# Embedding products in pairs of tiles, with whole-row stores from ACT's queue and earlier weight loads, in a one-layer hybrid decoder step

## The chip, the core and the metric

The kernel is one program on one core of a Trainium2 chip. The metric is the device time of an execution in microseconds (us): 1110.36 as the median of three runs (1109.34 to 1111.5). The engines are PE (matrix products; its weight loads are shown as PEld), DVE (vector), ACT (scalar, with a queue of its own for starting DMAs), POOL, and SP, which only starts DMAs. Each engine takes its instructions strictly in the order in which the program lists them. An instruction whose input or buffer isn't ready holds up everything behind it on its engine.

## What is computed

```python
h = rms_norm(x, norm_pre);  z = h @ w_in                     # 1024 -> 3584
a_out = silu(sg) * (gelu(u) * (W_s @ layer_norm(gelu(v)) + b))  # "S": chunks of 128 positions
b_out = silu(rg) * group_norm(retention(rotary(q), rotary(k), v))  # "R0", "R1": two heads each
mix = concat(a_out, b_out) @ w_out                            # "C1"
x = x + rms_norm(mix, norm_post)
x = x + sigmoid(x @ w_ple_gate) * (p @ w_ple_proj)            # "C2"; p @ w_ple_proj is "P"
```

There are 16 tiles of 128 prompt tokens and one tile of 64 sample tokens. The embedding p has 256 columns, so the product p @ w_ple_proj of a tile is small: two halves of 512 output columns, each of two blocks of 128 rows of p. Every fp32 operand is split into a rounded part (hi) and the rest (lo), and each block is three products (hi·hi, hi·lo, lo·hi). That is 12 products per prompt tile, each 128x128 by 128x512.

## The kernel before

The program is written as one long list of PE products. A counter goes up with each product, and everything else (loads, splits, copies, stores) is entered in the engines' orders at a given count. Stages follow each other on PE: S (all tiles), then P for the first nine tiles (eight of the prompt and the sample tile), R0 (pairs of tiles, seven groups of 12 products per pair: m1, m5, u2, c12, u3, c21, c11), P for the other eight tiles, R1 (as R0), C1, C2. The two P stretches are spoken of below as the first and the second stage boundary.

Names that matter:

- `z` are four PSUM banks used in turn. Each half of a P tile (6 products) takes one, and ACT copies it out (line 1163). A product into the fifth bank waits for the copy of the first.
- `slot` is a ring of 101 buffers of 2 KB per partition, for weights, operands and results alike. `bt` (function `block_rows`) is a pool of two buffers of 4 KB per partition, used before only in C1.
- A P tile's half is copied to a `slot` buffer P and stored from SP's queue (`store`, 12 products after the copy is entered) to `pleD`, 256 KB each. Its input p comes by one load per tile (line 1117), is cast by ACT (line 1130) and its rest is taken by DVE (line 1132).
- `fill` enters a weight's load some products ahead of its split (`lag`), ACT's rounding (lines 230 and 232) and DVE's rest (lines 239 and 241).
- In S, the v part of a tile goes through gelu (lines 376, 378, 380, 382), statistics (396, 398), POOL (401, 402), a scaling on DVE (404), the norm weight on POOL (406), and then four casts on ACT (420). `sgu_batch` mixes four tiles and stores them with `scatter` (16 small DMAs per batch, 64 KB each).
- Lines 936 and 939 take the products of R0 and R1 out of their banks.
- `cs` holds cosines and sines of a tile, loaded by one DMA per tile (line 1034).

Each DMA, whichever queue starts it, signs off on one of eight counters, taken in turn over the whole program. A DMA waits until the one eight places before it has landed.

Of the kernel before, what the change touches and what calls it, by code (L numbers as in the profile page):

```python
# [12 lines left out]
F32 = mybir.dt.float32  # L13
# [94 lines left out]
def hybrid_step(ctx: ExitStack, tc: tile.TileContext, a: dict):  # L108
# [12 lines left out]
    def name(s):  # L121
        uid[0] += 1
        return f"{s}_{uid[0]}"

    def slot(label, shape, dt=F32):

        return ring.tile(shape, dt, tag="slot", name=name(label))
# [10 lines left out]
    def t1k(shape, dt=F32):  # L138
        return slot("t1", shape, dt)
# [58 lines left out]
    def scatter(dst, src, n, qu=None, lag=LAG_D):  # L198


        def go(q):
            (qu or SY).dma_start(  # L202
                out=dst[q].rearrange("(b c) k r -> c b k r", b=4), in_=src[32 * q : 32 * q + 32]
            )

        for q in range(n // 32):
            st.later(lag + 3 * q, lambda q=q: go(q))
# [180 lines left out]
    def s_post(t, part, bank):  # L388
# [4 lines left out]
        if part == 0:  # L393
# [10 lines left out]
            V.tensor_scalar(out=w, in0=w, scalar1=mv[:, 0:1], scalar2=fc, op0=ALU.subtract, op1=ALU.mult)  # L404
            yield 2
            GP.tensor_tensor(out=w, in0=w, in1=sgu["ln"][0:n], op=ALU.mult)  # L406
            yield 7
            if t == SAMPLE:
                store(a["o_sguv"], w)
                sbatch["v", b] = w  # L410
# [40 lines left out]
    def sgu_batch(b):  # L451
# [22 lines left out]
        for h in range(2):  # L474
            yield 2
            for i in range(2):
                bt = blocks(t2k([P, 512]), [us[h][c][:, i, :] for c in range(2)], P)
                scatter(mixT[4 * b + 2 * h + i][:, :, 0:4, :], bt, P)
                yield 3

    def sgu_sample(uu):
# [352 lines left out]
    class Fast:  # L834
# [4 lines left out]
        def __init__(self, tiles, tab, source, post, begin, order):  # L839
            self.tiles, self.tab, self.source, self.post_, self.begin_ = tiles, tab, source, post, begin  # L840
            self.order = order
            self.sample = tiles[0] == SAMPLE
            self.raw, self.ops = {}, {}
            self.length = (32 if self.sample else 84)
# [176 lines left out]
    class FastR(Fast):  # L1021
# [7 lines left out]
            return (r_vg, r_qk)[part](t, self.pr, src, True)  # L1029

        def load(self):
            for t in self.tiles:
                cs = work.tile([P, P], F32, tag="cs", name=name("cs"), bufs=5)
                SY.dma_start(out=cs[0 : np_(t)], in_=a["cs"][t, 0 : np_(t)])
                ret["cs", t] = cs

        def prep(self):
            if self.sample:
# [68 lines left out]
    class Ple:  # L1107
        first = False

        def __init__(self, t, tab):  # L1110
            self.t, self.tab, self.raw, self.ops = t, tab, {}, {}
            self.length = 8 if t == SAMPLE else 12

        def load(self):
            t = self.t
            self.p = t1k([P, 2, P])[:, :, 0 : np_(t)]
            SY.dma_start(out=self.p, in_=(a["psT"] if t == SAMPLE else a["pT"][t]))

        def prep(self):
            p = self.p  # L1120
            if self.t == SAMPLE:
                pc = t1k([P, 2, P], F32R)
                S.copy(out=pc[:, :, 0:TS], in_=p)
                yield 2
                V.tensor_tensor(out=pc[:, :, TS:P], in0=p, in1=f(pc[:, :, 0:TS]), op=ALU.subtract)
                self.ops["p"] = [(pc,)]
            else:
                z = slot("A", [P, 2, 2, P], F32R)
                ph, pl = z[:, 0], z[:, 1]
                S.copy(out=ph, in_=p)  # L1130
                yield 2
                V.tensor_tensor(out=pl, in0=p, in1=f(ph), op=ALU.subtract)
                self.ops["p"] = [(ph, pl)]

        def begin(self):
            pass
# [4 lines left out]

        def main(self):
            seq = []
            for g in range(2):
                bank = [None]

                def first(bank=bank):
                    self.need("p")
                    bank[0] = zbank()

                mms = main_mms(self.t, _Lazy(self.ops, "p"), self.tab, g, range(2), bank)
                seq += [(lambda c=mms[0], first=first: (first(), c()), None)] + [(c, None) for c in mms[1:]]
                seq[-1] = (seq[-1][0], lambda g=g, bank=bank: st.start(self.post(g, bank[0])))
            return seq

        def post(self, g, bank):
            n = np_(self.t)
            if self.t == SAMPLE:
                out = yield from result_of(self.t, bank)
            else:  # L1160
                yield 1
                out = slot("P", [P, 512])
                S.copy(out=out, in_=bank)
            store(pleD[self.t][:, 512 * g : 512 * g + 512], out[0:n])


    c2 = {}
# [151 lines left out]
    unitsC1 = [Unit("C", [t], tabC1) for t in list(range(12)) + [SAMPLE] + list(range(12, NT))]  # L1319
    unitsC2 = [Fast(p, tabC2, x2T, c2_post, c2_begin, STEADY if 0 < j < 7 else ORDER) for j, p in enumerate(pairs)]  # L1320
    unitsC2.insert(4, Fast([SAMPLE], tabC2, x2T, c2_post, c2_begin, ORDER))
    unitsP = [Ple(t, tabP) for t in order]
    units = unitsS + unitsP[:9] + unitsR0 + unitsP[9:] + unitsR1 + unitsC1 + unitsC2

    begin, c = {}, 0
    for u in units:
# [3 lines left out]
    with tc.manual_schedule(engines={ENG.PE, ENG.SP, ENG.Activation, ENG.DVE, ENG.Pool}):  # L1330
# [42 lines left out]
        first8 = lambda u2: [begin[u2] + 12 * j for j in range(8)]  # L1373
        last = begin[unitsS[-1]]
        fill(stepsP, [last - 20 + 12 * j for j in range(4)])
        fill(stepsR0, [last - 24 * (8 - j) for j in range(8)] + [last + 28 + 10 * j for j in range(20)], 24)
        for j in range(NT // 2):
            st.start(spill_sums(j), 200 + 104 * j)
            st.start(spill_weights(j // 4, j % 4), 240 + 200 * j if j < 4 else 1540 + 90 * (j - 4))
        last = begin[unitsR0[-2]]  # L1380
        fill(stepsR1, [last - 25 * (6 - j) for j in range(6)] + [last + 34 + 10 * j for j in range(22)], 24)
        fill(stepsP, [last + 84 + 8 * j for j in range(4)])
        last = begin[unitsR1[-2]]
        fill(stepsC1, [last - 60 + 20 * j for j in range(5)] + [last + 46 + 8 * j for j in range(11)], 20)
# [142 lines left out]
```

## Time and profile before

| what | value |
|---|---|
| median of 3 runs | 1110.36 us |
| profiled execution | 1108.41 us, span 1106.6 us |
| PE / PEld busy | 1078.3 / 894.3 us (97% / 81%) |
| DVE / ACT / POOL busy | 811.2 / 501.0 / 357.8 us |
| granted clock, mean | 0.993 |
| chain that ended last | PE 86%, DVE 4%, DMA 4% |
| DMA | 253.55 MB, mean 229 GB/s |

In the table, busy is the time in which an engine executes something. The granted clock is TensorE's, as a share of full speed. The span leaves 28.3 us in which PE is not busy; 6.5 us of these lie behind the last product. The rest are a few gaps at the three places where one stage ends and another begins (about 280 to 345, 510 to 570 and 740 to 760 us).

### The profile page before, as it was taken

How to read it: one execution, taken by the hardware profiler on the slowest of the kernel's cores; microseconds unless marked ns; L12 is line 12 of the kernel's file. 1: busy time of each engine (PE TensorE's matmuls, PEld its weight loads, DVE VectorE, ACT ScalarE, POOL GpSimd, SP SyncE). 2: the span in 40 equal slices, each digit the busy share in tenths (PEclk: the TensorE clock that was granted, in tenths of full speed). 3: DMA queues.
4: the chain of work that ended last, by engine and by line, in shares of the span. 5: the costliest groups of instructions: out<-in, count | busy, mean ns of one | idle time of the engine just before them, and what ended most of it. 6: DMA issues, size and time to landing. Idle time of an engine off the chain costs nothing.

```text
span 1106.6 us, 16497 instructions
## 1 busy us (share of the span) xinstructions
PE 1078.3 (97%) x5028; PEld 894.3 (81%) x5028; DVE 811.2 (73%) x1512; ACT 501.0 (45%) x1042; POOL 357.8 (32%) x570
## 2 busy tenths in 40 slices
PE   9999999999898999999899999998999999999997
PEld 7888887888687888887778888886788888888886
DVE  4887687787755677879555666796678888986885
ACT  6664454654653334535543233353333244444442
POOL 5755454655301233333212323343355411000000
PEclk9999999999999999999999999999999999999999
DMA  9754867775597678897886656776768677865854
GB/s 309 242 195 152 290 233 222 258 266 162 186 321 247 220 241 269 287 286 211 271 268 197 193 171 209 233 218 186 228 217 264 190 226 229 268 216 193 282 162 143
DMA packets 227224, 253.55 MB, mean 229 GB/s; under 512 B 39104, under 2 KB 132800, under 8 KB 227136
## 3 DMA queue, kind: packets, MB, share of 16 engines
q1 hardware_dynamic: 217632, 243.85, 68.7%
q10 hardware_dynamic: 9504, 8.65, 2.7%
q8 instruction: 40, 0.66, 0.2%
q14 instruction: 48, 0.39, 0.1%
HBM read 172.86 MB, written 79.56 MB: 228 GB/s over the span
## 4 chain that ended last, share of the span: by engine, by line
PE 86%; DVE 4%; DMA 4%; ACT 2%; SPq 2%; issue 1%; POOL 1%; ACTq 0%; DVEq 0%; POOLq 0%
PE z L212 67%; PE s L212 19%; DMA t<-qkT 2%; SPq L202 1%; DMA W<-w_in 1%; DMA W<-wT 1%; DVE W L239 1%; DMA A<-xS10l 0%; ACT W L230 0%; DMA X<-xT 0%; DVE W L241 0%; POOL t L406 0%; DVE t L194 0%; DVE C L978 0%; DVE C L973 0%
## 5 line engine op out<-in xcount | busy, mean ns | idle before, releaser
L212 PE MATMUL z<-W,A 128*128 128x512 f32 x3632 | 897.7, 396 | 13.4 <-ACT C L936 5.2
L212 PEld LDWEIGHTS z<-W,A 128*128 128x128 f32 x3632 | 682.3, 189 | 155.2 <-ACT C L936 6.5
L212 PE MATMUL s<-W,A 128*128 128x512 f32 x672 | 184.3, 403 | 0.0
L212 PEld LDWEIGHTS s<-W,A 128*128 128x128 f32 x672 | 124.6, 189 | 21.4
L936 ACT COPY C<-z 128x512 f32<-128x512 f32 x96 | 56.2, 586 | 153.8 <-PE z L212 152.2
L529 POOL TENSOR_TENSOR t<-t,t 128x256 f32<-128x256 f32 (+1 forms) x34 | 28.5, 837 | 223.8 <-DVE t L526 103.5
L212 PEld LDWEIGHTS s<-t,t 128*128 128x128 f32 (+1 forms) x400 | 73.6, 186 | 12.4 <-issue 2.7
L212 PE MATMUL s<-t,t 128*128 128x128 f32 (+2 forms) x400 | 76.2, 272 | 0.0
L241 DVE SCALAR_TENSOR_TENSOR W<-W,c_npre,W 128x512 fp32r<-128x512 f32 x48 | 40.0, 845 | 41.2 <-ACT W L232 35.2
L863 DVE TENSOR_TENSOR A<-X,A 128x512 fp32r<-128x512 f32 (+1 forms) x78 | 54.0, 694 | 15.0 <-ACT A L861 14.8
L939 DVE TENSOR_TENSOR C<-z,C 128x512 f32<-128x512 f32 x48 | 33.1, 690 | 42.4 <-ACT C L936 26.7
L194 DVE STREAM_TRANSPOSE t<-t 128x512 f32<-128x512 f32 (+3 forms) x69 | 39.4, 573 | 27.0 <-POOL t L530 15.5
L555 ACT ACTIVATE t<-C,rsall 128x128 f32<-128x128 f32 (+1 forms) x68 | 23.6, 395 | 75.4 <-DVE C L939 68.0
L861 ACT CAST A<-X 128x512 fp32r<-128x512 f32 (+1 forms) x78 | 46.9, 602 | 4.5 <-DMA wT<-W 1.4
L603 POOL TENSOR_TENSOR t<-t,t 128x256 f32<-128x256 f32 (+1 forms) x34 | 29.5, 868 | 51.0 <-DVE t L598 43.0
L290 ACT CAST A<-X 128x512 fp32r<-128x512 f32 (+1 forms) x62 | 37.1, 600 | 19.4 <-issue 5.4
L1182 ACT ACTIVATE C<-C 128x512 f32<-128x512 f32 (+1 forms) x34 | 21.3, 633 | 50.4 <-DVE C L939 47.3
L239 DVE TENSOR_TENSOR W<-W,W 128x512 fp32r<-128x512 f32 x48 | 34.5, 722 | 10.6 <-ACT W L230 10.3
L292 POOL TENSOR_TENSOR A<-X,A 128x512 fp32r<-128x512 f32 (+1 forms) x28 | 39.3, 1424 | 5.2 <-ACT A L290 5.2
L232 ACT ACTIVATE W<-W,c_npre 128x512 fp32r<-128x512 f32 x48 | 33.8, 719 | 14.3 <-DMA W<-w_in 13.2
L422 POOL TENSOR_TENSOR v<-t,v 128x128 fp32r<-128x128 f32 x64 | 33.6, 547 | 16.1 <-ACT v L420 16.1
L380 ACT ACTIVATE t<-t,rsall 128x512 f32<-128x512 f32 (+1 forms) x34 | 24.2, 722 | 31.4 <-DVE t L378 31.4
(143 smaller groups left out, 1351.3 us busy)
## 6 DMA issues: line engine op xcount, KB each, us to landing
X<-xT SPq DMA_DIRECT2D x106, 256.0 KB, 4.2
W<-w_in SPq DMA_DIRECT2D x80, 256.0 KB, 4.9
X<-x SPq DMA_DIRECT2D x64, 256.0 KB, 4.2
qkT<-t SPq DMA_DIRECT2D x132, 64.0 KB, 2.0
x2T<-bt ACTq DMA_DIRECT2D x66, 128.0 KB, 3.7
wT<-W SPq DMA_DIRECT2D x32, 256.0 KB, 4.6
W<-wT SPq DMA_DIRECT2D x32, 256.0 KB, 3.9
ple<-P SPq DMA_DIRECT2D x32, 256.0 KB, 4.7
```

The lines of the kernel that those rows point to most:

```text
L194: V.transpose(out=by_k[:, k : k + nk], in_=part.rearrange("p (k b r) -> p k b r", b=4, r=32))
L212: PE.matmul(out, lhsT=l, rhs=r, start=start, stop=stop, skip_group_check=again)
L232: S.activation(out=hi, in_=raw, func=AF.Copy, scale=sc)
L239: V.tensor_tensor(out=lo, in0=raw, in1=f(hi), op=ALU.subtract)
L241: V.scalar_tensor_tensor(out=lo, in0=raw, scalar=sc, in1=f(hi), op0=ALU.mult, op1=ALU.subtract)
L290: S.copy(out=hi, in_=r)
L292: eng.tensor_tensor(out=lo, in0=r, in1=f(hi), op=ALU.subtract)
L422: GP.tensor_tensor(out=los[q][:, :, t % 4, :], in0=i, in1=f(o), op=ALU.subtract)
L861: S.copy(out=hi, in_=raw)
L863: V.tensor_tensor(out=lo, in0=raw, in1=f(hi), op=ALU.subtract)
L936: S.copy(out=c[key], in_=banks[b])
L939: V.tensor_tensor(out=c[key], in0=banks[b], in1=c[key], op=ALU.add)
```

## The change

Five edits are made together.

1. P works in pairs of tiles: one load, one cast and one subtraction for two tiles (512 KB, 128x512 per instruction). The PE order stays as it was, product for product.
2. The two halves of a P tile are copied into one buffer of the `bt` pool and stored with one DMA of whole rows (512 KB) that ACT's queue starts. The sample tile stays as before.
3. One load of `cs` per pair of tiles (3 buffers of two tiles instead of 5 of one).
4. The weights of R0 and R1 are loaded 40 products ahead instead of 24.
5. In S the four casts of v are entered 14 products after POOL's step instead of 7, and the 16 `scatter` DMAs of the last batch are started by ACT, 30 products after their transposes instead of 12.

```diff
@@ s_post, sgu_batch
-            yield 7
+            yield 14
             if t == SAMPLE:
...
-                scatter(mixT[4 * b + 2 * h + i][:, :, 0:4, :], bt, P)
+                scatter(mixT[4 * b + 2 * h + i][:, :, 0:4, :], bt, P, *((S, 30) if b == 3 else ()))
@@ FastR.load
-            for t in self.tiles:
-                cs = work.tile([P, P], F32, tag="cs", name=name("cs"), bufs=5)
-                SY.dma_start(out=cs[0 : np_(t)], in_=a["cs"][t, 0 : np_(t)])
-                ret["cs", t] = cs
+            t, n, w = self.tiles[0], np_(self.tiles[0]), len(self.tiles)
+            cs = work.tile([P, 2, P], F32, tag="cs", name=name("cs"), bufs=3)
+            SY.dma_start(out=cs[0:n, 0:w], in_=a["cs"][t : t + w, 0:n].rearrange("t p c -> p t c"))
+            for i, t in enumerate(self.tiles):
+                ret["cs", t] = cs[:, i]
@@ Ple
+            self.p = slot("A", [P, 2, 2, P])
+            t = self.tiles[0]
+            SY.dma_start(out=self.p, in_=a["pT"][t : t + 2].rearrange("t p k c -> p t k c"))
...
-                z = slot("A", [P, 2, 2, P], F32R)
-                ph, pl = z[:, 0], z[:, 1]
-                S.copy(out=ph, in_=p)
+                hi, lo = slot("A", [P, 2, 2, P], F32R), slot("A", [P, 2, 2, P], F32R)
+                S.copy(out=hi, in_=p)
                 yield 2
-                V.tensor_tensor(out=pl, in0=p, in1=f(ph), op=ALU.subtract)
-                self.ops["p"] = [(ph, pl)]
+                V.tensor_tensor(out=lo, in0=p, in1=f(hi), op=ALU.subtract)
+                for i, t in enumerate(self.tiles):
+                    self.ops[t] = [(hi[:, i], lo[:, i])]
...
-                out = slot("P", [P, 512])
-                S.copy(out=out, in_=bank)
-            store(pleD[self.t][:, 512 * g : 512 * g + 512], out[0:n])
+            yield 1
+            if g == 0:
+                self.out[t] = block_rows(P)
+            out = self.out[t]
+            S.copy(out=out[:, 512 * g : 512 * g + 512], in_=bank)
+            if g:
+                store(pleD[t], out, S)
@@ main part
-    unitsP = [Ple(t, tabP) for t in order]
-    units = unitsS + unitsP[:9] + unitsR0 + unitsP[9:] + unitsR1 + unitsC1 + unitsC2
+    unitsP = [Ple(p, tabP) for p in pairs]
+    unitsP.insert(4, Ple([SAMPLE], tabP))
+    units = unitsS + unitsP[:5] + unitsR0 + unitsP[5:] + unitsR1 + unitsC1 + unitsC2
...
-        fill(stepsR0, [last - 24 * (8 - j) for j in range(8)] + [last + 28 + 10 * j for j in range(20)], 24)
+        fill(stepsR0, [last - 24 * (8 - j) for j in range(8)] + [last + 28 + 10 * j for j in range(20)], 40)
...
-        fill(stepsR1, [last - 25 * (6 - j) for j in range(6)] + [last + 34 + 10 * j for j in range(22)], 24)
+        fill(stepsR1, [last - 25 * (6 - j) for j in range(6)] + [last + 34 + 10 * j for j in range(22)], 40)
```

ACT's order at the first boundary before, from the copy of the first P half on. A row is a line of the kernel, the operation, result and inputs; in brackets stand the counters that it waits for (PE, DVE, ACT's own, and DMAHW0 to 7, the eight counters of the DMAs).

```order
L1163 COPY P_3559<-z_3539 128x512 [waits PE_49]
L1130 CAST A_3562<-t_665_3481 128x256 [waits DMAHW7_49]
L1163 COPY P_3575<-z_3557 128x512 [waits PE_49,Activation_49]
L232 ACTIVATE W_3582<-W_3522,c_npre 128x512 [waits DMAHW2_49]
L1163 COPY P_3591<-z_3573 128x512 [waits PE_49]
L1130 CAST A_3594<-t_671_3518 128x256 [waits DMAHW1_49,Activation_49]
L1163 COPY P_3606<-z_3586 128x512 [waits PE_49]
L232 ACTIVATE W_3609<-W_3544,c_npre 128x512 [waits DMAHW3_49]
L1163 COPY P_3622<-z_3603 128x512 [waits PE_49]
```

Every copy waits for PE alone, since each has a new buffer of the ring. The same place now, from the third half on (`bt_3582`, `bt_3608` and `bt_3636` are the rows of the second, third and fourth tile; ple_222 is signed off on counter 5, ple_223 on counter 1):

```order
L1172 COPY bt_3582<-z_3566 128x512 [waits PE_49]
L185 DMA ple_222<-bt_3553 128x1024 [waits Activation_49]
L1172 COPY bt_3582<-z_3578 128x512 [waits PE_49]
L232 ACTIVATE W_3594<-W_3499,c_npre 128x512 [waits DMAHW0_49]
L1172 COPY bt_3608<-z_3589 128x512 [waits DMAHW5_49,PE_49]
L1135 CAST A_3611<-A_3538 128x512 [waits DMAHW2_49]
L230 CAST W_3619<-W_3524 128x512 [waits DMAHW1_49]
L185 DMA ple_223<-bt_3582 128x1024 [waits Activation_49]
L1172 COPY bt_3608<-z_3606 128x512 [waits PE_49]
L1172 COPY bt_3636<-z_3623 128x512 [waits DMAHW1_49,PE_49]
```

The stores have moved into ACT's order, each behind the first copy of the tile after next. From the third tile on, the first copy of a tile waits for the landing of the store of the tile two before it.

SP's order at the first boundary before, from the load of the last p of the stretch on:

```order
L1117 DMA t_688_3578<-pT 128x256 [waits DMAHW6_49,PE_49]
L185 DMA ple_222<-P_3559 128x512 [waits DMAHW7_49,Activation_49]
L223 DMA W_3598<-wT_196 128x512 [waits DMAHW0_49,PE_49]
L185 DMA ple_222<-P_3575 128x512 [waits DMAHW1_49,Activation_49]
L1117 DMA t_698_3611<-psT 128x2x64 [waits DMAHW2_49,PE_49]
```

The stores of P stood there among the loads, each waiting for ACT's copy; now there is none of them on SP. ACT's order now where R0 begins (`mixT` are the small DMAs of the last S batch, `C_3889` is the copy of m1's bank):

```order
L202 DMA mixT_104<-t_733_3761 32x4x128 [waits DMAHW1_49]
L202 DMA mixT_105<-t_738_3775 32x4x128 [waits DMAHW2_49]
L232 ACTIVATE W_3882<-W_3767,c_npre 128x512
L202 DMA mixT_106<-t_742_3789 32x4x128 [waits DMAHW3_49]
L202 DMA mixT_107<-t_748_3806 32x4x128 [waits DMAHW4_49,DVE_49]
L202 DMA mixT_105<-t_738_3775 32x4x128 [waits DMAHW5_49]
L936 COPY C_3889<-z_3849 128x512 [waits PE_49,Pool_49]
```

Before, these 16 DMAs stood on SP. Eleven of them now stand on ACT ahead of m1's copy, and five behind it.

## Rows read from the trace of the kernel before

**Rows 1.** Timeline of PE, 255 to 345 us (start, duration, [idle before <-releaser])

```profile
298.16 9.35 PE L212 MATMUL z<-W,A 128*128 128x512 f32 x33 [4.18 <-DVE t L382]
...
323.76 8.32 PE L212 MATMUL z<-W,A 128*128 128x512 f32 x36
333.06 3.01 PE L212 MATMUL z<-W,A 128*128 128x512 f32 x12 [0.97 <-ACT C L936]
338.18 4.62 PE L212 MATMUL z<-W,A 128*128 128x512 f32 x12 [2.10 <-ACT C L936]
```

**Rows 2.** Windows: PE, PEld, DVE, ACT, POOL busy, granted clock, DMA share, GB/s

```profile
280.00:300.00 20.00, 15.82 (x67) 12.74 (x66) 16.71 (x28) 12.72 (x30) 8.63 (x13) 0.95 0.49 169
300.00:320.00 20.00, 20.00 (x97) 16.82 (x96) 14.27 (x37) 12.90 (x27) 0.00 (x0) 0.96 0.92 324
...
520.00:540.00 20.00, 15.46 (x66) 12.05 (x67) 14.30 (x31) 11.91 (x26) 5.15 (x6) 0.91 0.75 215
540.00:560.00 20.00, 17.89 (x80) 14.46 (x79) 8.60 (x23) 9.74 (x18) 3.85 (x8) 0.94 1.02 356
```

**Rows 3.** Timeline of ACT, 270 to 345 us

```profile
295.27 0.30 ACT L420 CAST v<-t 128x128 fp32r<-128x128 f32 x1 [3.18 <-POOL t L406]
295.47 0.72 ACT L380 ACTIVATE t<-t,rsall 128x512 f32<-128x512 f32 x1
...
300.08 0.58 ACT L1163 COPY P<-z 128x512 f32<-128x512 f32 x1
300.56 0.73 ACT L232 ACTIVATE W<-W,c_npre 128x512 fp32r<-128x512 f32 x1
301.19 0.57 ACT L1163 COPY P<-z 128x512 f32<-128x512 f32 x1
...
331.81 0.72 ACT L232 ACTIVATE W<-W,c_npre 128x512 fp32r<-128x512 f32 x1 [4.54 <-DMA W<-w_in]
332.44 0.57 ACT L936 COPY C<-z 128x512 f32<-128x512 f32 x1
```

**Rows 4.** Waits of SP's queue, 280 to 302 us (total, times, longest)

```profile
SPq L185 <- ACT A L1130: 13.3, 1, 13.3
```

**Rows 5.** Timeline of SP, 270 to 345 us

```profile
286.45 0.38 SPq L1117 DMA_DIRECT2D t<-pT  x1
299.90 0.33 SPq L185 DMA_DIRECT2D ple<-P  x1
```

**Rows 6.** Timeline of PE, 540 to 572 us

```profile
556.94 10.09 PE L212 MATMUL z<-W,A 128*128 128x512 f32 x36 [2.11 <-ACT C L936]
```

**Rows 7.** Timeline of ACT, 505 to 575 us

```profile
528.15 0.58 ACT L1163 COPY P<-z 128x512 f32<-128x512 f32 x1
...
553.81 0.41 ACT L543 COPY t<-t 128x256 f32<-128x256 f32 x1 [4.85 <-DMA t<-qkT]
...
556.31 0.58 ACT L936 COPY C<-z 128x512 f32<-128x512 f32 x1
```

**Rows 8.** Timeline of PE, 740 to 765 us

```profile
750.45 0.49 PE L212 MATMUL s<-t 128*128 128x128 f32 x2 [3.34 <-ACT t L543]
```

**Rows 9.** DMA issues, 272.5 to 277 us (operation, count, size, median us to landing)

```profile
xS37h<-A SPq DMA_DIRECT2D x1, 256.0 KB, 2.0
```

**Rows 10.** DMA issues, 524 to 546 us

```profile
ple<-P SPq DMA_DIRECT2D x9, 256.0 KB, 3.3
```

**Rows 11.** DMA issues of the whole span

```profile
ple<-P SPq DMA_DIRECT2D x32, 256.0 KB, 4.7
```

**Rows 12.** Tile bt: DMA issue on ACT's queue (duration in ns, min/median/max)

```profile
L202 ACTq DMA_DIRECT2D x2T<-bt x66: 309/385/758, 767.4 to 953.9; - x66
```

**Rows 13.** Groups by form (count, busy us, mean ns, idle before)

```profile
L420 ACT CAST v<-t 128x128 fp32r<-128x128 f32 x64 | 15.7, 293 | 34.4 <-POOL t L406 34.4
L230 ACT CAST W<-W 128x512 fp32r<-128x512 f32 x48 | 29.5, 618 | 7.5 <-DMA W<-wT 2.9 <-DVE W L239 2.4 <-DMA W<-w_out 1.1
L1130 ACT CAST A<-t 128x256 fp32r<-128x256 f32 x16 | 6.4, 402 | 0.0
```

More of the change, by code (lines that the diff above doesn't have):

```diff
@@ L1108, in hybrid_step, with __init__ @@
         first = False
-        def __init__(self, t, tab):
-            self.t, self.tab, self.raw, self.ops = t, tab, {}, {}
-            self.length = 8 if t == SAMPLE else 12
+        def __init__(self, tiles, tab):
+            self.tiles, self.tab, self.ops, self.out = tiles, tab, {}, {}
+            self.sample = tiles[0] == SAMPLE
+            self.length = 8 if self.sample else 12 * len(tiles)
         def load(self):
-            t = self.t
-            self.p = t1k([P, 2, P])[:, :, 0 : np_(t)]
-            SY.dma_start(out=self.p, in_=(a["psT"] if t == SAMPLE else a["pT"][t]))
+            if self.sample:
+                self.p = t1k([P, 2, P])[:, :, 0:TS]
+                SY.dma_start(out=self.p, in_=a["psT"])
+                return
+            self.p = slot("A", [P, 2, 2, P])
+            t = self.tiles[0]
+            SY.dma_start(out=self.p, in_=a["pT"][t : t + 2].rearrange("t p k c -> p t k c"))
         def prep(self):
             p = self.p
-            if self.t == SAMPLE:
+            if self.sample:
                 pc = t1k([P, 2, P], F32R)
@@ L1125, in prep @@
                 V.tensor_tensor(out=pc[:, :, TS:P], in0=p, in1=f(pc[:, :, 0:TS]), op=ALU.subtract)
[L1126 removed]
+                self.ops[SAMPLE] = [(pc,)]
             else:
[L1128 to L1130 removed]
+                hi, lo = slot("A", [P, 2, 2, P], F32R), slot("A", [P, 2, 2, P], F32R)
+                S.copy(out=hi, in_=p)
                 yield 2
[L1132 to L1133 removed]
+                V.tensor_tensor(out=lo, in0=p, in1=f(hi), op=ALU.subtract)
+                for i, t in enumerate(self.tiles):
+                    self.ops[t] = [(hi[:, i], lo[:, i])]
         def begin(self):
@@ L1143, in main, with first, post @@
             seq = []
[L1144 to L1153, printed above, removed]
-            return seq
[L1156 to L1161, printed above, removed]
-                out = slot("P", [P, 512])
-                S.copy(out=out, in_=bank)
-            store(pleD[self.t][:, 512 * g : 512 * g + 512], out[0:n])
+            for t in self.tiles:
+                for g in range(2):
+                    bank = [None]
+                    def first(t=t, bank=bank):
+                        self.need(t)
+                        bank[0] = zbank()
+                    mms = main_mms(t, _Lazy(self.ops, t), self.tab, g, range(2), bank)
+                    seq += [(lambda c=mms[0], first=first: (first(), c()), None)] + [(c, None) for c in mms[1:]]
+                    seq[-1] = (seq[-1][0], lambda t=t, g=g, bank=bank: st.start(self.post(t, g, bank[0])))
+            return seq
+        def post(self, t, g, bank):
+            if self.sample:
+                out = yield from result_of(t, bank)
+                store(pleD[t][:, 512 * g : 512 * g + 512], out)
+                return
+            yield 1
[5 more added lines that the diff above has]
+                store(pleD[t], out, S)
     c2 = {}
```

## The prediction

> **What bounds the kernel now.** I read the page first. PE is busy for 97% of the span, and the chain that ended last is 86% PE, so only PE's gaps and slow stretches can be won. PE's timeline then showed where they are: at three stage boundaries.
>
> At the first boundary PE stands still three times, for 4.18, 0.97 and 2.10 us [rows 1]. After the first wait 33 products take 9.35 us. The 36 products later take 8.32 us (0.227 each, with 0.17 of tail), so 33 should take 7.5: PE ran part of them at 1.2 GHz, and the granted clock of that window is 0.95 to 0.96 [rows 2]. After the third wait 12 products take 4.62 us, where 12 took 3.01 [rows 1]. Such a low stretch costs 1.6 to 1.9 us behind a wait. At the second boundary the last wait is 2.11 us, and the 36 products behind it take 10.09 us [rows 6]. At the third one wait is 3.34 us [rows 8].
>
> ACT's timeline tells why. The 4.18 us wait is for line 382, whose input comes from the tanh of line 380. That tanh stood behind a cast of line 420 which waited 3.18 us for POOL [rows 3]. Then SP: it issued nothing from 286.45 to 299.90, as its next DMA was the first store of P and waited 13.3 us for ACT [rows 4, 5]. The loads behind it came late: at 331.81 a weight's rounding on ACT had waited 4.54 us for its load, and the copy of R0's bank stood behind it [rows 3]. That is PE's wait of 0.97, and the 2.10 is the same again. At the second boundary a copy of line 543 waited 4.85 us for its load, ahead of m1's copy at 556.31 [rows 7].
>
> **The change part by part.** The change takes away the causes just named: no store of P on SP, the casts of line 420 behind the tanh, loads further ahead. What it puts in their place has to be priced. PE's order is the same, so the sum is a shift of a few points of that order.
>
> *Two row buffers.* A P tile now needs a `bt` buffer from its first copy until its store has landed, and there are two. On ACT, in order: first copy of tile i+2 (waits for the landing of store i), one or two casts, store i+1, second copy of i+2, first copy of i+3 (waits for store i+1), and so on. Store i+1 stands behind the copy that waits for store i, so the landings follow one another and can't overlap: six landings from store 0 to the first copy of tile 7. I call one landing D, from issue to the buffer's release.
>
> First boundary. Before, the third half's copy began at 301.19 [rows 3], and store 0 is now issued right behind it. The tanh of line 380 no longer waits, which moves this row by about 0.6 (0.72 for the tanh that goes first, less what the casts behind it take over): 300.6. Between the landings ACT has 1.5, 1.0, 0.8, 1.5 and 0.5 us of copies and casts that can't be hidden (0.5 each when they follow closely, by the starts 300.08 and 300.56 [rows 3]): 5.3. So tile 7's first copy begins at 300.6 + 5.3 + 6D = 305.9 + 6D. From there to m1's copy ACT has three more copies, two casts, one rounding at 0.63, 13 DMA issues at 0.43 (0.385 and a gap [rows 12]) and the copy itself: 2.0 + 1.0 + 0.6 + 5.6 + 0.6 = 9.8. Eleven of the 13 are the `mixT` DMAs. u2 can't begin before that copy: 315.7 + 6D. Then u2, c12 and u3 at 2.72 each, 0.6 for m5's copy behind five more issues, and one low-clock stretch of 1.9 as after such waits before: u3 ends at 326.4 + 6D. Before, u3 ended at 338.18 + 4.62 = 342.8 [rows 1]. The shift is 6D - 16.4.
>
> Second boundary. Store 0 is issued at 528.7, behind the third copy at 528.15 [rows 7]; nothing ahead of it changes much. Between the landings stand 1.0, 1.0, 1.0, 1.5 and 0.5: tile 7's first copy at 533.7 + 6D. Then two copies, two issues and two roundings, and m1's copy, 3.7 in all: u2 at 537.4 + 6D. Before, u2 began at 556.94 [rows 6], and I let the low clock behind it stand. The shift is 6D - 19.5.
>
> Together 12D - 35.9. It is zero at D = 2.99 us, and every 0.1 us of D is 1.2 us.
>
> *What D is.* No row shows a store of 512 KB. From below: 256 KB landed in 2.0 us with the queues nearly empty [rows 9], so D isn't under 2.0. From above: the median of P's stores is 4.7 us [rows 11], where SP kept the DMAs full (share 0.92 [rows 2]). The nearest row is P's stores at the second boundary, with SP's loads beside them: 3.3 us [rows 10]. The second 256 KB cost 0.7, at the 350 GB/s that 324 GB/s at a share of 0.92 make for a full share [rows 2], so 4.0 if nothing else changed. But in this chain SP is held too, since its eighth DMA behind a store waits for that store; DMAs are emptier than there. I take D = 3.5, nearer to 4.0 than to the idle row's 2.0 + 0.7 = 2.7. The sum is 42.0 - 35.9 = +6.1.
>
> The Trainium skill ("DMA: Bandwidth & Descriptors", section "Anatomy of one DMA") fits a DMA as 2.0 us plus its bytes at 436 GB/s, measured on GpSimd's path: an estimate of 3.2 us for 512 KB and, by the same sum, +2.5 us. For 256 KB it gives 2.6, while the rows here have 2.0 idle and 3.3 to 4.7 loaded, so the trace agrees with it only in the middle. The rule that speaks against the change is in "Perfetto Trace Analysis", section "Identifying the Most-Contended Engine": the same gap again and again on the engine that should be full can mean too few buffers. PE's gaps before are single ones [rows 1, 6]; by that rule the change would make them a row of equal ones, as the forecast has it.
>
> *The rest.* 16 casts of 402 ns become 8 of about 618 [rows 13]: 1.5 us less of ACT, and about as much of DVE, beside waits. 16 loads of cosines, 8 of p and 32 stores fewer on SP, at 0.33 to 0.38 each [rows 5], save some 20 us of a queue that isn't what PE waits for any more at these places. Line 420's 34.4 us of waits [rows 13] are hidden by the z banks everywhere but at the 4.18 wait. Loads 40 products ahead hold ring slots 16 products (3.6 us) longer; the 20 buffers that P no longer takes from the ring at each boundary (12 for 32) cover that. All this I put at nothing, with 1 us either way. The third boundary's 3.34 [rows 8] comes from line 543's chain, which no edit touches.
>
> **Sum.** The profiled execution took 1108.4 us, 2.0 below the median of the runs. 1108.4 + 6.1 = 1114.5, and on the scale of the median 1116.5.
>
> **The rivals.**
>
> A. The stores land early enough, and PE sets the pace. For it: D = 2.7 from the idle row. Then tile 7's copy is ready when PE is. At the first boundary the tanh still leaves some 3 us of the first wait, and the `mixT` issues still hold m1's copy, so 4 to 6 of the waits and low clock go; at the second the 2.11 and its low stretch of 1.8 go. Some -9: 1101.5. Against it: DMA shares of 0.75 to 1.0 at both places [rows 2]. The Trainium skill ("DMA: Bandwidth & Descriptors", section "Rules for kernel authors") has merged transfers pay; by that rule alone A would be the outcome, and no run here has yet shown a store of this size.
>
> B. Worse than the chain: landings couple through the eight counters. SP's loads behind a store wait for it, and weights of R0 or R1 come late again, so that the roundings of rows 3 hold copies up once more. Price: D of 4.2 (+14.5), or the old 0.97 + 2.10 + 1.6 back on top of the forecast: about 1122 to 1125. It decides once a period of the chain moves more than the DMAs do in it: a store and three to five loads are 1.2 to 1.8 MB, 3.5 to 5 us at 350 GB/s, against a period of D + 1.
>
> C. D near 3.0: what the chain costs is what the old waits cost. 1110.
>
> D. The row buffers hardly matter, since the wait of ACT is shorter than the four z banks. Against it: the banks cover 5.4 us once, while the landings add up to 18 us and more over eight tiles that take PE 21.8.
>
> **How the numbers follow.** Forecast (D from 3.2 to 4.0) 0.50, B 0.17, C 0.12, A with D 0.21. Likeliest 1116.5, its own range 1112 to 1122. Taking in most of A and of B, the range is 1102 to 1129. A change of under 0.2% (2.2 us) can't be told from none here. Faster 0.21, same 0.13, slower 0.66.
>
> **What would show it.** In the profile after: ACT copies of line 1172 with DMA `ple<-bt` as the releaser, some 2 to 3 us each and five or six in a row at both boundaries; PE's waits there for that line; `ple<-bt` x16 of 512 KB at 3 to 4 us to landing; SP's long wait and the wait for line 380 gone; m1's copy behind a row of `mixT` issues on ACT. The forecast is wrong if `ple<-bt` lands in under 2.9, if the copies wait for PE alone, or if PE's largest waits lie elsewhere.

## The result, and the profile after

The changed kernel takes 1115.64 us (median of five runs, 1113.75 to 1117.33) against 1109.63 for the kernel before in the same measurement (1107.16 to 1111.5). The ratio is 1.0054, with a 95% interval of 1.0035 to 1.0073: slower by 6.0 us, where 6.1 were forecast. The profiled execution took 1115.95 us with a span of 1114.1, so it lies 7.5 us over the profiled one of before. The total came out as forecast; its parts did not all do so.

First the page of the kernel after: the chain that ended last by lines, PE's largest group with the idle time ahead of it, and the new stores (count, size, median us to landing).

```profile
PE z L212 66%; PE s L212 18%; DMA ple<-bt 3%; DMA W<-w_in 1%; DMA t<-qkT 1%; DMA mixT<-t 1%; DVE W L239 1%; DMA X<-xT 0%; DMA A<-xS46h 0%; DMA cs<-cs 0%; DMA t<-xT 0%; DVE W L241 0%; DVE C L939 0%; DVE C L978 0%; DVE C L973 0%
...
L212 PE MATMUL z<-W,A 128*128 128x512 f32 x3632 | 899.8, 397 | 13.0 <-ACT bt L1172 5.7
...
ple<-bt ACTq DMA_DIRECT2D x16, 512.0 KB, 4.5
```

The stores stand in the chain with 3% of the span, and what PE waits for most in this group is the copy of P's banks. A store lands in 4.5 us, against 4.7 for the halves of before over the whole span [rows 11].

The waits of the kernel after, of PE and then of ACT (total us, times, longest):

```profile
PE s L212 <- ACT t L543: 9.2, 5, 3.3
PE z L212 <- ACT bt L1172: 7.5, 5, 2.5
PE z L212 <- ACT C L936: 3.2, 3, 1.4
PE z L212 <- DVE t L382: 2.4, 1, 2.4
...
ACT bt L1172 <- DMA ple<-bt: 23.4, 9, 3.8
```

The wait for line 382 is 2.41 us where it was 4.18 [rows 1], and the waits for line 936 are shorter. In their place stand 7.5 us for line 1172, behind ACT's 23.4 us for landings. SP's wait of 13.3 us for ACT [rows 4] is gone, but SP isn't free: it now stands for landings of stores, since each DMA waits for the one eight places before it. Its queue's waits that end between 298 and 345 us, the kernel after:

```profile
SPq L1058 <- DMA ple<-bt: 11.6, 3, 4.2
SPq L1054 <- DMA ple<-bt: 9.5, 1, 9.5
SPq L223 <- DMA ple<-bt: 4.2, 1, 4.2
SPq L185 <- DMA ple<-bt: 3.4, 1, 3.4
```

They add up to 28.7 us. The 9.5 us end at 302.46, just behind the landing of the first store, which ACT issued at 299.75; before, SP's long wait ended at 299.90 [rows 5]. Now ACT's timeline at the first boundary after, from store 1 to m1's copy; rows of ACTq are DMA issues.

```profile
303.13 0.59 ACT L1172 COPY bt<-z 128x512 f32<-128x512 f32 x1 [0.24 <-PE z L212]
303.14 0.33 ACTq L185 DMA_DIRECT2D ple<-bt  x1
...
308.01 0.59 ACT L1172 COPY bt<-z 128x512 f32<-128x512 f32 x1 [2.77 <-DMA ple<-bt]
308.12 0.33 ACTq L185 DMA_DIRECT2D ple<-bt  x1
308.50 0.62 ACT L230 CAST W<-W 128x512 fp32r<-128x512 f32 x1
309.01 0.59 ACT L1172 COPY bt<-z 128x512 f32<-128x512 f32 x1
309.49 0.63 ACT L230 CAST W<-W 128x512 fp32r<-128x512 f32 x1
312.69 0.59 ACT L1172 COPY bt<-z 128x512 f32<-128x512 f32 x1 [2.56 <-DMA ple<-bt]
312.79 0.33 ACTq L185 DMA_DIRECT2D ple<-bt  x1
...
326.80 0.59 ACT L1172 COPY bt<-z 128x512 f32<-128x512 f32 x1 [2.99 <-DMA ple<-bt]
...
333.79 0.72 ACT L232 ACTIVATE W<-W,c_npre 128x512 fp32r<-128x512 f32 x1 [3.79 <-DMA mixT<-t]
...
335.34 0.59 ACT L936 COPY C<-z 128x512 f32<-128x512 f32 x1 [0.82 <-DVE W L241]
```

One landing releases one copy, and 0.1 us after the copy starts the next store goes out: 308.12, 312.79, and so on, five times. The casts between them lie inside the wait for the landing, since the copy that waits stands behind them. PE's timeline there, the kernel after:

```profile
297.02 9.47 PE L212 MATMUL z<-W,A 128*128 128x512 f32 x33 [2.41 <-DVE t L382]
...
322.85 2.11 PE L212 MATMUL z<-W,t 128*128 128x512 f32 x8 [1.76 <-ACT bt L1172]
327.44 7.38 PE L212 MATMUL z<-W,A 128*128 128x512 f32 x24 [2.47 <-ACT bt L1172]
335.98 3.04 PE L212 MATMUL z<-W,A 128*128 128x512 f32 x12 [1.16 <-ACT C L936]
339.65 5.74 PE L212 MATMUL z<-W,A 128*128 128x512 f32 x24 [0.63 <-ACT C L936]
```

The rows answer to those of before [rows 1]. The 24 products at 327.44 took 7.38 us where 24 take 5.6 to 5.7, so part of them ran at 1.2 GHz (the granted clock between 320 and 340 us is 0.91); behind 335.98 there is no such stretch. Further on in the kernel after, late in R0, at the second and at the third boundary, PE again:

```profile
506.34 0.71 PE L212 MATMUL s<-t 128*128 128x128 f32 x2 [2.04 <-ACT t L543]
...
526.41 3.49 PE L212 MATMUL z<-W,A 128*128 128x512 f32 x14 [0.69 <-DVE W L239]
...
557.48 5.73 PE L212 MATMUL z<-W,A 128*128 128x512 f32 x24 [0.88 <-ACT bt L1172]
564.65 8.46 PE L212 MATMUL z<-W,A 128*128 128x512 f32 x36 [1.45 <-ACT C L936]
...
756.55 0.79 PE L212 MATMUL s<-t 128*128 128x128 f32 x2 [3.34 <-ACT t L543]
757.85 7.17 PE L212 MATMUL z<-W,A 128*128 128x512 f32 x21
```

In R0 there is a wait of 2.04 us that before did not have, with a low stretch behind it (the pair behind the wait takes 0.71, the one at 750.45 in before 0.49; the granted clock between 506 and 512 us is 0.72). At the second boundary u2 starts 7.7 us later than before [rows 6], but its 36 products take 8.46 and not 10.09. At the third the wait is the same 3.34 us [rows 8]; 21 products behind it take 7.17, where in the timeline of PE before they took 5.04:

```profile
751.15 5.04 PE L212 MATMUL z<-W,A 128*128 128x512 f32 x21
```

### The profile page after: what moved, and what is told of

Read it like the earlier page. It is cut to its first block, busy times and chain, and to the rows that moved or that the text cites. A ratio compares the mean times of both kernels' runs of the same rounds, so it can differ in the third digit from the quotient of the medians.

```text
span 1114.1 us, 16390 instructions
## 1 busy us (share of the span) xinstructions
PE 1082.4 (97%) x5028; PEld 896.0 (80%) x5028; DVE 815.6 (73%) x1504; ACT 500.4 (45%) x1034; POOL 364.0 (33%) x570
## 4 chain that ended last, share of the span: by engine, by line
PE 85%; DMA 8%; DVE 4%; ACT 1%; issue 1%; SPq 0%; ACTq 0%; POOL 0%; DVEq 0%; POOLq 0%
PE z L212 66%; PE s L212 18%; DMA ple<-bt 3%; DMA W<-w_in 1%; DMA t<-qkT 1%; DMA mixT<-t 1%; DVE W L239 1%; DMA X<-xT 0%; DMA A<-xS46h 0%; DMA cs<-cs 0%; DMA t<-xT 0%; DVE W L241 0%; DVE C L939 0%; DVE C L978 0%; DVE C L973 0%
## 5 line engine op out<-in xcount | busy, mean ns | idle before, releaser
L422 POOL TENSOR_TENSOR v<-t,v 128x128 fp32r<-128x128 f32 x64 | 36.3, 596 | 19.1 <-ACT v L420 19.1
```

Of the source, the lines that this page charges most:

```text
L422: GP.tensor_tensor(out=los[q][:, :, t % 4, :], in0=i, in1=f(o), op=ALU.subtract)
```

## Where the time stands, place by place

For each kernel I took six points of PE's timeline that the unchanged order lets one find again: the start of the first wait at boundary 1 (293.98 in before), the first product of two small operands in R0 (354.47), the wait for line 239 at the end of R0 (519.93), the first small product behind boundary 2 (590.48), the wait of 3.34 (750.45) and the end. The table has what each kernel lost (+) or won (-) against the profiled execution of before between two points, in us. It is one execution of each; the runs of one kernel spread over 3 to 8 us (12 in E10), so single entries under 2 us mean little, and columns more than entries.

| kernel | ahead | boundary 1 | R0 | boundary 2 | rest | sum |
|---|---|---|---|---|---|---|
| after | +0.63 | +1.91 | +3.94 | -0.39 | +1.41 | +7.50 |
| E1, lead 24 | +0.25 | +2.91 | -0.03 | +3.84 | +1.63 | +8.60 |
| E2, four row buffers | +0.41 | -0.89 | +5.12 | -2.59 | +2.25 | +4.30 |
| E3, pairs of P alone | -0.03 | +2.64 | +2.17 | +1.35 | +0.47 | +6.60 |
| E4, all but the pairs | +0.13 | -1.07 | +2.57 | -3.87 | +0.64 | -1.60 |
| E5, halves in the ring | +0.62 | -1.86 | +2.00 | -3.30 | +0.54 | -2.00 |
| E6, half-row stores | +0.24 | +1.74 | +3.05 | +1.19 | +0.58 | +6.80 |
| E7, E4 and split lead | +0.27 | -3.78 | +4.13 | -3.47 | -0.25 | -3.10 |
| E8, E4 and 98 slots | +0.41 | -3.18 | +3.29 | -3.07 | +2.05 | -0.50 |
| E9, E4 and lead 24 | +0.22 | -1.18 | +1.34 | -2.21 | +0.23 | -1.60 |
| E10, E6 and mixT on SP | +0.60 | -0.47 | +6.15 | +1.84 | +0.18 | +8.30 |
| E11, E7 and 102 slots | 0.00 | -3.50 | +0.87 | -2.66 | +0.29 | -5.00 |
| E12, E5, split lead, 102 | +0.02 | -3.12 | +4.12 | -3.43 | -0.29 | -2.70 |

What R0's column is made of can be read from the traces. PE's waits of over 0.1 us for line 543 there add up to 1.0 us in before, 0.9 in E1, 3.4 in after and 1.7 to 5.2 in the others. In after, line 543 itself had waited for a load of `qkT`:

```profile
505.67 0.62 ACT L543 COPY t<-t 128x512 f32<-128x512 f32 x1 [3.19 <-DMA t<-qkT]
```

The rest of after's +3.94, about 1.6 us, is the low stretch behind 506. A wait near 499 to 506 us (0.64 to 2.04) stands in all ten kernels that load R0's weights 40 products ahead, and in none of the four with 24 (before, E1, E3, E9). So this wait comes with the longer lead, and what E4 over E9, and after over E1, lose in R0 (1.2 and 4.0 us) they get back at boundary 2 (1.7 and 4.2). An earlier wait, near 475 to 483 us, stands in all fourteen (0.76 to 2.37); why it varies is not shown.

## The experiments

My theory after the result was the forecast's: two row buffers make the landings follow one another, and that is the price. The rival was that the other edits, above all the longer lead, cost what is seen in R0, and that the row buffers are beside the point. Each kernel was timed in five rounds beside the kernel before; us of difference are the ratio less one, times 1109.6. E9 to E12 ran on another chip than E1 to E8, so that the two groups are compared by their ratios alone.

**E1.** The lead of the weights' loads back at 24.

```diff
-... [last + 28 + 10 * j for j in range(20)], 40)
+... [last + 28 + 10 * j for j in range(20)], 24)
-... [last + 34 + 10 * j for j in range(22)], 40)
+... [last + 34 + 10 * j for j in range(22)], 24)
```

> The kernel after with the weights' loads 24 products ahead again. Theory 1 (the longer lead costs in R0): a load of W that waits for a ring buffer stood ahead of the qkT DMAs on SP at 485.59 to 488.18, they came 5 us late, and PE's wait of 2.04 us at 506.34 with the low clock behind it (1.8) follows from that. Then that wait goes and the median is 1115.6 - 3.8 = 1111.8 (1110.8 to 1112.8); the waits of ACT for ple<-bt stay near 23 us. Theory 2 (all of the loss is the two row buffers, and the wait in R0 is only a late start handed on): 1115.6, 0.7 either way, with the wait in place.

Measured: 1115.07 us, ratio 1.0061 (1.0045 to 1.0078). The wait at 506 is gone from its trace, as theory 1 had it, but the time is not: boundary 2 gave the same amount back (+3.84 for -0.39 in the table). R0 ended 3.35 us sooner than in after (523.06 for 526.41), but the landings took longer (28.1 us for the first six at boundary 2, 25.8 in after), and tile 7's first copy came at 561.10 for 561.82. By the time, theory 2 has it, though the wait that it expected in place is gone: the lead makes the wait in R0, but it is no cause of the loss as a whole.

**E2.** Four row buffers for two, and a ring of 98 slots for 101 to make room.

```diff
-SLOTS = 101
+SLOTS = 98
-        return work.tile([P, D], F32, tag="bt", name=name("bt"), bufs=2)[0:n]
+        return work.tile([P, D], F32, tag="bt", name=name("bt"), bufs=4)[0:n]
```

> The kernel after with four row buffers in place of two (ring of 98 slots in place of 101, for the room). Theory 1 (two row buffers make the landings follow one another): ACT's 23.4 us of waits for ple<-bt fall under 3, PE's waits for line 1172 go, u3 ends 3 to 5 us sooner than 345.2, and the time is 1111 to 1113; the wait in R0 stays. Theory 2 (m1's copy is held by the mixT DMAs and by late loads whatever the buffers): 1115, 1 either way.

Measured: 1112.31 us, ratio 1.0029 (1.0017 to 1.0042), 2.8 us better than after, though a store now lands in 5.0 us. Both boundaries are better than before. ACT's waits of line 1172 for a landing are gone; one of 1.7 us, ahead of line 333, is left. PE's waits in this kernel:

```profile
PE s L212 <- ACT t L543: 9.1, 7, 3.4
PE z L212 <- ACT C L936: 5.6, 3, 3.1
PE z L212 <- DVE t L382: 3.6, 1, 3.6
PE z L212 <- ACT bt L1172: 2.4, 2, 1.8
```

The 2.4 us for line 1172 stand ahead of the chain at boundary 2, where after has them too (0.64 and 1.73 at 530 to 534), and none at boundary 1. So the landings still take as long, but they overlap. What is left of the loss stands in R0, and E8 shows that the smaller ring costs by itself.

**E3 and E4.** The pairs of P with their row buffers alone, and all other edits without them.

E3, against before (with the rest of class `Ple` as in the change):

```diff
-    unitsP = [Ple(t, tabP) for t in order]
+    unitsP = [Ple(p, tabP) for p in pairs]
...
+                store(pleD[t], out, S)
```

E4, against before (with both lines of `fill`):

```diff
-            yield 7
+            yield 14
...
-                scatter(mixT[4 * b + 2 * h + i][:, :, 0:4, :], bt, P)
+                scatter(mixT[4 * b + 2 * h + i][:, :, 0:4, :], bt, P, *((S, 30) if b == 3 else ()))
...
-            for t in self.tiles:
-                cs = work.tile([P, P], F32, tag="cs", name=name("cs"), bufs=5)
+            t, n, w = self.tiles[0], np_(self.tiles[0]), len(self.tiles)
+            cs = work.tile([P, 2, P], F32, tag="cs", name=name("cs"), bufs=3)
...
-        fill(stepsR0, ..., 24)
+        fill(stepsR0, ..., 40)
```

> The kernel before with the products of P in pairs and whole-row stores on ACT's queue alone (cosines, casts of line 420, mixT on SP and the lead of 24 as before). Theory 1: the chain of landings is there (ACT waits over 20 us for ple<-bt), no wait of 2 us in R0; the first wait of boundary 1 is 4 us again; 1112 to 1114. Theory 2 (row buffers harmless, the loss is in the other edits): 1109 or less.

> The kernel before with all edits but the pairs of P: cosines per pair, casts of line 420 later, mixT of the last batch on ACT, loads 40 ahead. Theory 1 (the lead costs 3.8 in R0, the tanh that no longer waits gives back about 1.8 at boundary 1): 1111 to 1113. Theory 2 (these edits help and the row buffers alone cost): 1105 to 1108.

Measured: E3 1117.22 us, ratio 1.0077 (1.0065 to 1.009), slower than foreseen by either theory; E4 1106.27 us, ratio 0.9979 (0.9966 to 0.9992), theory 2. The edits of P cost 8.5 us by themselves, and 8.3 on top of the others (1.0054 less 0.9979). The other edits gain 2.3 us by themselves. In E3 ACT waits 23.3 us for `ple<-bt`, as in after.

**E5.** After, with each half of P copied to a buffer of the ring again and stored by itself, from ACT's queue.

```diff
-            if g == 0:
-                self.out[t] = block_rows(P)
-            out = self.out[t]
-            S.copy(out=out[:, 512 * g : 512 * g + 512], in_=bank)
-            if g:
-                store(pleD[t], out, S)
+            out = slot("P", [P, 512])
+            S.copy(out=out, in_=bank)
+            store(pleD[t][:, 512 * g : 512 * g + 512], out, S)
```

> The kernel after with P's halves copied to buffers of the ring again, as before, and stored one by one (256 KB) from ACT's queue: pairs and queue as in after, no row buffers. Theory 1 (the two row buffers are the price, 2.8 us at boundary 1 and 2 to 3.5 at boundary 2, by the difference of after and of the kernel with all other edits): no wait for ple<-bt, boundary 1 as there, 1108 to 1111. Theory 2 (the stores on ACT's queue or the loads by pairs cost as much): 1113 to 1116.

Measured: 1108.7 us, ratio 1.0003 (0.9991 to 1.0015): theory 1. Pairs, casts, queue and order are those of after, and the loss is gone. At boundary 1 the stores land hardly faster than the whole rows did in after (4.2 us in the median, 4.5 there):

```profile
ple<-P ACTq DMA_DIRECT2D x16, 256.0 KB, 4.2
```

but no copy waits for them. SP does: 19.7 us for `ple<-P` in the same stretch, where it was 28.7 for `ple<-bt` in after, so that these waits of SP don't make the loss by themselves. The loss that went is 5.7 us by the ratios. E5 changes two things, the buffers and the size of a store; E6 takes them apart.

**E6.** After, with each half row stored as soon as it is copied.

```diff
-            if g:
-                store(pleD[t], out, S)
+            store(pleD[t][:, 512 * g : 512 * g + 512], out[:, 512 * g : 512 * g + 512], S)
```

> The kernel after with its two row buffers, but each half row stored as soon as it is copied (two DMAs of 256 KB for one of 512 KB, both on ACT's queue). Theory 1 (a release costs one landing D, and 12 of them count): the last store of a tile is smaller, D falls from 4.4 to about 3.3, ACT's waits for ple<-bt from 23 us to under 14, and the time to 1110 to 1113. Theory 2 (the DMAs are full, so a release takes as long whatever the split): 1114 to 1117, waits of 20 us and more.

Measured: 1115.08 us, ratio 1.0056 (1.004 to 1.0071). D fell as theory 1 had it, and ACT's waits with it, from 23.4 us to 16.3; the time did not follow, as theory 2 had it, though for another reason. ACT at boundary 1 in this kernel:

```profile
324.21 0.59 ACT L1172 COPY bt<-z 128x512 f32<-128x512 f32 x1 [0.85 <-DMA ple<-bt]
...
332.48 0.72 ACT L232 ACTIVATE W<-W,c_npre 128x512 fp32r<-128x512 f32 x1 [5.06 <-DMA mixT<-t]
...
334.16 0.59 ACT L936 COPY C<-z 128x512 f32<-128x512 f32 x1 [0.96 <-DVE W L241]
```

Its stores, of the page's DMA issues:

```profile
ple<-bt ACTq DMA_DIRECT2D x32, 256.0 KB, 3.3
```

Tile 7's first copy comes 2.6 us sooner than in after, m1's copy only 1.2: the `mixT` DMAs on ACT's queue, each behind an earlier DMA, now hold it for 5.06 us.

E6 and E5 differ in the buffers alone: both store 256 KB at a time from ACT's queue, after the same pairs and casts. E6 loses 5.9 us against E5 by the ratios, and the intervals are apart. Together they show the two row buffers as the cause of this loss, and not the size of the stores.

**E7 and E8.** E4 with R1's first six loads at 24 ahead and the others at 40, and E4 with a ring of 98.

```diff
-        fill(stepsR1, [last - 25 * (6 - j) for j in range(6)] + [last + 34 + 10 * j for j in range(22)], 40)
+        fill(stepsR1[:6], [last - 25 * (6 - j) for j in range(6)], 24)
+        fill(stepsR1[6:], [last + 34 + 10 * j for j in range(22)], 40)
```

```diff
-SLOTS = 101
+SLOTS = 98
```

> The kernel with all edits but the pairs of P (1106.3), with the first six loads of R1's weights at 24 products ahead, the others at 40. Theory 1 (the wait of 2 us near 503 comes from these six, which stand on SP waiting for ring buffers ahead of the qkT DMAs; the gain at boundary 2 comes from the others): R0's waits fall from 3.4 to about 1 us and the time to 1103 to 1105. Theory 2 (the gain at boundary 2 needs the six early loads too, or the wait in R0 comes from elsewhere): 1106 or more.

> The same kernel (all edits but the pairs of P, 1106.3) with a ring of 98 slots in place of 101, as the kernel with four row buffers had. Theory 1 (the pairs of P and ACT's queue cost the rest of that kernel's 6 us): 1106 to 1107.5. Theory 2 (the smaller ring costs, since loads wait for slots): 1109 to 1112, with more wait in R0.

Measured: E7 1105.0 us, ratio 0.9967 (0.9953 to 0.998), the best of all by its ratio, within theory 1's span of times. But its reason falls: R0's waits rose from 3.4 to 4.9 us, and the gain over E4 (1.3 us, the intervals overlap) is not shown. E8 1110.51 us, ratio 1.0015 (1.0005 to 1.0025): theory 2. Three slots less cost 4.0 us against E4 by the ratios; its one profile was a quick execution, 0.5 below before, and doesn't say where. E2 has the same ring and lies 1.6 us over E8 (the intervals overlap). So with four row buffers the pairs of P cost about what they cost without any (2.7 us, E5 over E4), and not the 8.3 of two; most of E2's 3.2 us over before can be laid to the ring. No run has four row buffers and 101 slots.

**E9.** E4 with the lead at 24: cosines, later casts and `mixT` on ACT alone.

```diff
-        fill(stepsR0, ..., 40)
+        fill(stepsR0, ..., 24)
...
-        fill(stepsR1, ..., 40)
+        fill(stepsR1, ..., 24)
```

> The kernel before with cosines per pair, casts of line 420 later and mixT of the last batch on ACT; the lead stays at 24 and the pairs of P are left out. Theory 1 (these three give back the tanh's wait at boundary 1, about 1.8 us, and the lead of 40 brings as much at boundary 2 as it costs in R0): 1106 to 1108. Theory 2 (the 3 us that all edits but the pairs gain come from the longer lead): 1109 to 1110, as before.

Measured: 1107.36 us, ratio 0.9995 (0.9982 to 1.0009). In theory 1's span, but not told apart from no change. With E1 and after: the longer lead gains 1.8 us without the pairs and 0.8 with them, each less than its uncertainty.

**E10.** E6 with the `mixT` DMAs on SP's queue.

```diff
-                scatter(mixT[...][:, :, 0:4, :], bt, P, *((S, 30) if b == 3 else ()))
+                scatter(mixT[...][:, :, 0:4, :], bt, P)
```

> The kernel after with half-row stores from its two row buffers (1115.1, its landings 3.3 us), and the mixT DMAs of the last batch on SP's queue again. Theory 1 (with shorter landings it is these DMAs on ACT, with a wait of 5.1 us ahead of m1's copy, that keep u2 from starting sooner): u2 starts at 330 to 332 in place of 334.8 and the time is 1111 to 1113. Theory 2 (late loads of weights hold the roundings ahead of m1's copy wherever these DMAs stand): u2 at 334 to 335.5, 1114 to 1116.

Measured: 1113.34 us (1106.39 to 1118.68), ratio 1.0044 (1.0024 to 1.0063). At the place named, theory 1 is right: m1's copy comes at 329.41 in place of 334.16, and PE goes on to u2 without a wait. Then ACT stands still for the next late thing, an x tile's load, and m5's copy behind it:

```profile
329.41 0.59 ACT L936 COPY C<-z 128x512 f32<-128x512 f32 x1
...
337.19 0.62 ACT L861 CAST A<-X 128x512 fp32r<-128x512 f32 x1 [5.47 <-DMA X<-xT]
337.71 0.58 ACT L936 COPY C<-z 128x512 f32<-128x512 f32 x1
```

By the time it is unclear: 1.3 us better than E6, with intervals that overlap, and the median lies between the two theories' spans. The profiled execution (1116.72) is 3.4 us above this median.

**E11 and E12.** E7, and E5 with E7's split lead, each with a ring of 102 slots.

```diff
-SLOTS = 101
+SLOTS = 102
```

> The kernel with all edits but the pairs of P and R1's first six loads at 24 ahead (1105.0), with a ring of 102 slots in place of 101. Theory 1 (a slot of the ring is worth over 1 us, as the 4.2 us for three fewer have it): 1102.5 to 1104. Theory 2 (101 are enough; the loss at 98 is a threshold): 1105, 1 either way.

> The kernel after with P's halves in the ring and stored from ACT's queue (1108.7), R1's first six loads at 24 ahead and a ring of 102 slots. Theory 1 (the rest of its distance to the kernel without pairs, 2.4 us, is pressure on the ring): 1104 to 1106. Theory 2 (it is ACT's queue, with 32 more DMAs on it): 1107 to 1109.

Measured: E11 1104.86 us, ratio 0.9974 (0.996 to 0.9987), no different from E7: one slot more is worth nothing that can be seen, theory 2. E12 1107.32 us, ratio 0.9994 (0.9979 to 1.0009), 2.2 us over E11, as E5 was 2.7 over E4: theory 2 by its size. So pairs of P without row buffers may still cost about 2 us, at the edge of what the intervals tell; whether by ACT's queue, the larger loads or the casts of two tiles at once was not taken apart.

## Why the prediction was right, and where it was not

*The mechanism* was right at boundary 1. The copies of line 1172 wait for `ple<-bt`, 2.6 to 3.0 us each and five in a row, and PE waits for the copies. E5 and E6, which differ in the row buffers alone, have the loss gone and in place. Each store goes out with the first copy of the next tile, as the forecast's chain has it and the order printed with the change shows (not of the tile after next, as the sentence below that order says): store 1 at 303.14, with the third tile's copy at 303.13.

At boundary 2 the landings followed one another only in part. ACT waited four times for a landing (0.22, 3.83, 2.50 and 2.92 us); in between, the fourth tile's first copy waited for PE, and the fifth's stood behind a copy of line 543 that waited for its load. The kernel after:

```profile
540.85 0.59 ACT L1172 COPY bt<-z 128x512 f32<-128x512 f32 x1 [1.38 <-PE z L212]
...
545.40 0.62 ACT L543 COPY t<-t 128x512 f32<-128x512 f32 x1 [2.60 <-DMA t<-qkT]
...
552.22 0.59 ACT L1172 COPY bt<-z 128x512 f32<-128x512 f32 x1 [3.83 <-DMA ple<-bt]
```

*SP's long wait* was to go. It only changed its releaser: SP stood 9.5 us for the first store, until it had landed, and 28.7 us for stores in all.

*The total* met the forecast, 6.0 us for 6.1, in part by luck. The forecast had +4.6 at boundary 1, +1.5 at boundary 2 and nothing elsewhere, 1 us either way. In the profiled executions boundary 1, with what stands ahead of it, is +2.5, boundary 2 is -0.4, and +5.3 lies elsewhere.

*D was mis-sized.* I took 3.5 us; the six that count at boundary 1 landed in 2.65 to 4.79, 4.26 in the mean, and at boundary 2 in 2.63 to 6.04, 4.3 in the mean. The step that failed is "DMAs are emptier than there": their share between 300 and 340 us was 0.78 to 0.79, and 0.81 in the stretch of before from which 3.3 us was read (524 to 546 us [rows 10]). That row was also a low one to start from: its nine stores take in three that landed in 2.0 to 2.5 us, while the seven of before that were issued from 547 us on took 4.9 to 5.7. The two windows of the kernel after (columns as in [rows 2]):

```profile
300.00:320.00 20.00, 20.00 (x96) 16.78 (x96) 12.30 (x32) 10.16 (x20) 0.00 (x0) 0.96 0.79 271
320.00:340.00 20.00, 13.98 (x51) 10.04 (x50) 6.39 (x12) 7.68 (x14) 0.00 (x0) 0.91 0.78 246
```

The Trainium skill's fit ("DMA: Bandwidth & Descriptors", section "Anatomy of one DMA") gives an estimate of 3.2; the trace has 2.65 for the first store and 4.5 in the median, so it agrees with neither.

*The work between landings was mis-sized the other way.* I put 5.3 us of copies and casts there. From the issue of store 0 at 299.75 to tile 7's first copy at 326.80 are 27.05 us, of which the landings make 25.56: 1.5 are left. At boundary 2 they are 27.92 us and 25.81, so 2.1 are left where I had 5.0. The casts run inside the wait for the landing, and ACT's queue starts the next store 0.1 us after the copy begins. At boundary 1 the two errors, with a store 0 that went out 0.85 us early, cancel: 326.8 measured, 305.9 + 21 = 326.9 forecast. That is luck.

*Boundary 1.* m1's copy came 8.5 us behind that copy, not 9.8, and u2 to u3 had no low stretch. u3 ended at 345.4 (339.65 + 5.74), not at 347.4: +2.6 us over before where +4.6 were forecast.

*Boundary 2.* Seen from the wait for line 239, 6.48 us late, u2 started at +7.71, so the boundary itself cost 1.2 us; 1.5 were forecast. I had let the low clock behind u2 stand; it was not there, and 1.6 us came back. The sum for the place was -0.4.

*The rest* was put at nothing, 1 us either way, and was +5.3: 3.9 in R0, and 1.4 from the third boundary on, which is the clock behind an unchanged wait less a second wait of before (1.14 us) that has gone. R0's part is PE's waits for line 543 and a low stretch, as told below the table; one of these waits comes with the longer lead, and why the other varies stays open. The part is there, with 0.9 to 6.2 us, in all profiles but E1's, with and without row buffers, with the lead at 24 (E3, E9) and at 40, and it is largest in several of those that came to R0 early (E7, E12). The profiled execution of before may simply be one with a quick R0. That would make the agreement of the place-by-place sum with the total partly chance, while E3, E4 and E5 stand on medians.

*The rule "0.1 us of D is 1.2 us" was wrong.* E6 took a quarter off D and gained nothing. It supposes that every landing at both boundaries is in the chain and that nothing else is late behind it; E6 and E10 show the next two, the `mixT` DMAs on ACT and the x loads, close behind.

*The rivals.* A (landings early, PE sets the pace) fell: the landings took 4.3 us. C fell likewise, and rival D by E5 and E6. B came nearer: its D of 4.2 was met, and so was its coupling, by which SP's loads wait for a store. Its 1122 was not, for the reason just told, and E5, where SP waits for stores too, loses nothing against before. One of the forecast's own signs of being wrong is half met: over the whole span PE waits longest for line 543 (9.2 us, 7.3 in before) and not for line 1172 (7.5).

The rule of the Trainium skill on gaps that come again and again ("Perfetto Trace Analysis", section "Optimization Strategy") holds here for ACT: too few buffers was the cause of its five equal waits, and E2 and E5 mend it from both ends. PE's own gaps for line 1172 are five of 0.6 to 2.5 us, and not the row of equal ones that the forecast expected.

The forecast's 6.1 is the chain less the old waits, and so it never named what the chain costs alone. By the medians that is 5.7 us (E5) to 5.9 (E6 against E5). In the profiled executions it is 6.7 at the boundaries, since boundary 1 has +1.9 in after and -1.9 in E5, boundary 2 -0.4 and -3.3.

## What to carry to other kernels

Before merging two stores into one larger one, count the buffers that it needs and ask when each is free again: with two buffers, landings of 4.3 us set the pace of ACT at boundary 1, however little work it had. Half the size in many buffers beat the full size in two, and half the size in two did not. And where a wait goes, look for the next late thing behind it: here three stood one behind the other, so that shortening the first (E6) moved m1's copy by 1.2 of 2.6 us, and the time by nothing that can be seen.

## What the runs showed of the hardware

ACT's queue starts a DMA while the engine computes: the issue at 299.75 lies inside an activation that runs from 299.62 to 300.35, and the store at 308.12 went out 0.11 us into the copy that begins at 308.01. The same half-row store of 256 KB from ACT's queue landed in 2.0 to 6.0 us between 298 and 330 us of E6. And the same wait of PE, 3.34 us at the third boundary, was followed by products at full speed in before and by a low stretch in after; these are the stretches from 754 to 764 us, first of before (PE, PEld, DVE, ACT, POOL busy, granted clock, DMA share, GB/s):

```profile
754.00:759.00 5.00, 3.86 (x22) 3.11 (x20) 1.44 (x2) 1.81 (x4) 1.40 (x3) 1.00 0.62 157
759.00:764.00 5.00, 5.00 (x26) 4.23 (x25) 3.30 (x9) 1.39 (x4) 2.11 (x3) 1.00 0.94 276
```

The same stretches of after, where the wait ends at 756.55:

```profile
754.00:759.00 5.00, 2.45 (x8) 2.17 (x9) 4.18 (x10) 2.81 (x7) 1.51 (x1) 0.66 0.02 6
759.00:764.00 5.00, 5.00 (x17) 3.94 (x16) 0.25 (x1) 0.53 (x2) 0.00 (x0) 0.65 0.52 134
```

The granted clock falls to 0.65 over these 10 us in after, which means 1.2 GHz for most of them, and stays at 1.00 in before. It cost 2.1 us over 21 products (7.17 against 5.04). What decides between the two is not shown here.
